# Two-layer hybrid decoder step: gate and halo tiles in a pool of their own, down pools exchanged, residual split and squares on VectorE alone, key transposes three tiles behind

## The chip, the cores and the metric

The kernel runs on one core of one Trainium2 chip. The metric is device time in microseconds (us) of one execution; lower is better. The core has a matrix engine (TensorE, PE in the profile, with weight loads PEld), VectorE (DVE), ScalarE (ACT), GpSimd (POOL) and a queue engine (SyncE, SP), which run side by side and wait for each other through semaphores. Each engine takes its own instructions strictly in order.

## The reference, cut to what matters

One inference step of a two-layer trunk, for a prompt of 1024 tokens and 64 sample tokens that share all weights. Layer 0 mixes tokens with a gated MLP and pooling, layer 1 with sliding-window attention; both then attend to 256 memory tokens and end in a convolutional feed-forward block:

```python
def rmsnorm(x, g):
    xf = x.astype(jnp.float32)
    y = xf * lax.rsqrt(jnp.mean(xf * xf, -1, keepdims=True) + EPS)
    return (y * g.astype(jnp.float32)).astype(x.dtype)

def conv_ffn(h, g_ctx, w_up, conv_w, conv_b, w_down):
    T = h.shape[1]
    up = h @ w_up
    g, u = up[..., :D_FF], up[..., D_FF:]
    g_ext = jnp.concatenate([g_ctx, g], 1)
    gc = conv_b
    for j in range(CONV_W):
        gc = gc + conv_w[j] * g_ext[:, j:j + T]
    y = (gelu(gc) * u) @ w_down
    return y, g_ext[:, -(CONV_W - 1):]

def swa_qkv(h, pos, w_qkv, q_gain, k_gain):
    N, T, _ = h.shape
    qkv = h @ w_qkv
    q = qkv[..., :N_HEADS * HEAD_DIM].reshape(N, T, N_HEADS, HEAD_DIM)
    k = qkv[..., N_HEADS * HEAD_DIM:(N_HEADS + N_KV) * HEAD_DIM].reshape(N, T, N_KV, HEAD_DIM)
    v = qkv[..., (N_HEADS + N_KV) * HEAD_DIM:].reshape(N, T, N_KV, HEAD_DIM)
    q = rope_partial(rmsnorm(q, q_gain), pos)
    k = rope_partial(rmsnorm(k, k_gain), pos)
    return q, k, v
```

D_MODEL is 1024, D_FF 2816, 16 query heads and 4 key heads of 64. The parts before and after these are not touched.

## The kernel before, in words

All 1088 tokens stay on the chip, features along partitions: 8 blocks of 128 features, by tokens in three chunks `c` of 384, 384 and 320 (`CHS`). Every fp32 operand is held as a high part (fp32r) and the remainder low part, and each product is three matmuls: high by high, high by low, low by high (L1016 to L1018 in the feed-forward block, L259 to L261 elsewhere). The residual stream lives in the tile `big`, as `xh` and `xl` for each chunk.

**Order.** TensorE's instructions stand in the order in which they are written. The other engines' instructions are put in order by the tile framework's scheduler from its own estimate, so an edit can move instructions that it does not name. A pool's tiles lie at fixed addresses in the on-chip memory (SBUF), and a new tile waits until the last users of the old tiles at its address are done.

**Feed-forward block (`ffn`).** The up projection and then the down projection run as seven-product block multiplications (`seven`, L1007): for each job seven products "1", "7", "5", "6", "4", "2", "3" in the PSUM tiles `psa` and `psb`, the products "7" and "4" of a job being run inside the next one, and at the very end alone. Between "7" and "4" the partial sum in PSUM must have been read out, since both use one tile. In the up phase the gate half goes through tiles `g` (convolution, with the two-column halo `hl`), `ge` holds the gelu, and `m` tiles hold partial results (11 buffers). Results go to DRAM tiles `hd` by SP's queue (L1250, L1255, L1256). Pools: `fg` has g, m and hl (L1135, L1193, L1219), `fge` has ge.

The down phase reads `hd` back, by POOL's queue: `load_b` (L1354 for the three parts stored split, L1357 for the four stored whole, which ScalarE and VectorE then split at L1358 and L1359). The first seven operand tiles lie in `big`, the next eight in the pool `db` (tiles `b`). The pool `de` holds `xr`, the old residual, loaded by SP at L1366. `de` is opened before `db`, so in SBUF `xr` takes the place of the first `g` tile, and the `b` tiles that of `g`, `m`, `hl` and `ge`. PSUM results are added to the new residual `x32` on VectorE at L1375 (named `x` in the profile).

**After the block of layer 0 (`after_ffn`, L1396).** For each chunk and feature block `split_x` copies the high part on ScalarE (L292), subtracts on GpSimd for even `m` and on VectorE for odd `m` (L293), squares on ScalarE (L303) and adds the square to `acc` on GpSimd for odd `m` and VectorE for even `m` (L305): 24 subtractions and 21 additions, 12 of each on GpSimd. While the down phase ends, VectorE also splits the first attention weights (L255 in `load_rows`).

**Attention of layer 1 (`swa`, L1445).** For each of nine token tiles `kv_tile` projects keys and values: 24 matmuls, then the norm's sum (`norm_tm`, L341, from `acc`), then on ScalarE the scaling (L1498) and squares (L618), on VectorE and GpSimd the head norm and rotary part (L620 to L625, L336, L1485 to L1488, tile `pT`). `trk(t - 2)` transposes the rotated keys of the tile two before on TensorE (L167), after the 18th matmul of tile t. Then come the query tiles (`q_tile`, tile `gq`): the first holds `trk(7)` in its middle, and `trk(8)` follows the second.

Of the kernel before, what the change touches and what calls it, by code (L numbers as in the profile page):

```python
# [9 lines left out]
F32 = mybir.dt.float32  # L10
F32R = mybir.dt.float32r
AF = mybir.ActivationFunctionType
ALU = mybir.AluOpType
# [10 lines left out]
HT = 544  # L24
# [47 lines left out]
def kernel(  # L72
# [10 lines left out]
    V, S, P, T = nc.vector, nc.scalar, nc.gpsimd, nc.tensor  # L83
    mm = T.matmul

    def pool(name, bufs=1, **kw):
        return tc.tile_pool(name=name, bufs=bufs, reuse_waits="tile", **kw)
# [7 lines left out]
    def f(ap):  # L95
        return ap.bitcast(F32)
# [176 lines left out]
    def proj_tm(ws, t, mid=None):  # L273
        c, o, w = tile_of(t)
        ps = psA()
        for k in range(KB):
            wt = ws[k // 2]
            mm3(ps[:w, :], xh[c][:, k, o:o + w], xl[c][:, k, o:o + w], wt[:, 0, k % 2, :], wt[:, 1, k % 2, :],
                k == 0, k == KB - 1)
            if k == 5 and mid:  # L280
                mid()
        return ps
# [4 lines left out]
    def new_acc(c, place):  # L287
        acc[c] = R["tmp"].tile([128, CHS[c][1]], F32, tag=f"acc{c}", name=f"acc{c}") if place is None else place

    def split_x(c, m, src, alt=False):  # L290
        n = CHS[c][1]
        S.activation(xh[c][:, m, :], src, AF.Copy)  # L292
        (P if alt and m % 2 == 0 else V).tensor_tensor(out=xl[c][:, m, :], in0=src, in1=f(xh[c][:, m, :]), op=ALU.subtract)  # L293
        squares(c, m, src)

    def squares(c, m, src, place=None, odd=1):
        n = CHS[c][1]
        if m == 0:
            new_acc(c, place)
            S.activation(acc[c], src, AF.Square)  # L300
        else:
            sq = tmp()
            S.activation(sq[:, :n], src, AF.Square)  # L303
            E = P if m % 2 == odd else V
            E.tensor_tensor(out=acc[c], in0=acc[c], in1=sq[:, :n], op=ALU.add)  # L305
# [815 lines left out]
    def ffn(l, xq, rvq, gtail, B0, factors, rs):  # L1121
# [10 lines left out]
        with ExitStack() as es:  # L1132
            bq = es.enter_context(tc.tile_pool(name=f"fb{l}", bufs=1, reuse_waits="tile", side="right"))
            B = [B0, {i: bq.tile([128, 2, 4, QT], F32R, name=f"b1{i}") for i in "1562374"}]
            gpp = es.enter_context(pool(f"fg{l}"))  # L1135

            def up_w(pair, up):
# [51 lines left out]
            def gate_out(pair, q):  # L1189
                hb = 2 * pair  # L1190
                g, t = [], {}
                for i in range(2):
                    gt = gpp.tile([128, 562], F32, tag="g", name="g", bufs=3)  # L1193
                    g.append(gt)

                def put(i, nh, a, b2):

                    def op(out, a_, b_):
                        if b_ is None:
                            S.activation(out, a_, AF.Copy)  # L1200
                        else:
                            V.tensor_tensor(out=out, in0=a_, in1=b_, op=ALU.add)

                    if nh == 0 or q == 0:
                        op(g[i][:, 2 + QT * nh:2 + QT * nh + QT], a, b2)
                    else:
                        op(g[i][:, 274:482], a[:, 0:208], b2[:, 0:208])
                        op(g[i][:, 482:562].rearrange("p (n r) -> p n r", r=10)[:, :, 2:10],
                           a[:, 208:272].rearrange("p (n t) -> p n t", t=8), b2[:, 208:272].rearrange("p (n t) -> p n t", t=8))

                def start(i):
                    if q == 0:
                        V.memset(g[i][:, 0:2], 0.0)
                    else:
                        V.tensor_copy(g[i][:, 0:2], halo.pop(hb + i))

                def done(i):
                    if q == 0:
                        hl = halo[hb + i] = gpp.tile([128, 2], F32, tag="hl", name="hl", bufs=4)  # L1219
                        V.tensor_copy(hl, g[i][:, 544:546])  # L1220
                    conv(hb + i, q, g[i])

                def out(what, ps):
                    if what in ("m1", "u2", "m5"):
                        t[what] = mtile()
                        S.activation(t[what], ps, AF.Copy)
                    elif what == "m2":
                        start(0)
                        put(0, 0, ps, t["m1"])
                    elif what == "m53":  # L1230
                        put(0, 1, ps, t["u2"])
                        done(0)
                    elif what == "u3":
                        start(1)
                        put(1, 1, ps, t["m5"])
                    else:
                        put(1, 0, ps, None)
                        done(1)

                return out  # L1240
# [87 lines left out]
        xpl = rs.enter_context(tc.tile_pool(name=f"x32{l}", bufs=1, reuse_waits="tile", side="right"))  # L1328
        x32 = [xpl.tile([128, KB, HT], F32, name=f"x32_{q}") for q in range(2)]
        with ExitStack() as es:  # L1330
            ep = es.enter_context(pool(f"de{l}"))
            bq = es.enter_context(pool(f"db{l}"))
            count = [0]

            def btile():
# [60 lines left out]
    def after_ffn(l, x32, conv_out):  # L1396

        conv_out(stage)
        for c, (o, n) in enumerate(CHS):
            for m in range(KB):  # L1400
                parts_ = [(q, max(o, HT * q), min(o + n, HT * q + HT)) for q in range(2)]
                parts_ = [p_ for p_ in parts_ if p_[1] < p_[2]]
                if len(parts_) == 1:
                    q, a, b = parts_[0]
                    split_x(c, m, x32[q][:, m, a - HT * q:b - HT * q], True)
                else:
                    t = tmp()[:, :n]
                    for q, a, b in parts_:
                        S.activation(t[:, a - o:b - o], x32[q][:, m, a - HT * q:b - HT * q], AF.Copy)
                    split_x(c, m, t, True)  # L1410

    def final(x32, conv_out):
        with ExitStack() as es:
# [31 lines left out]
    def swa(wkv):  # L1445
        sc = 64.0 ** -0.5
        with ExitStack() as es:
            bp = es.enter_context(pool("swa"))
            qo = bp.tile([128, 8, 1088], F32, name="qo")
            if True:  # L1450
# [41 lines left out]

                def kv_tile(t):
                    c, o, w = tile_of(t)
                    ps = proj_tm(wkv, t, (lambda: trk(t - 2)) if t > 1 else None)
                    rt[t] = norm_tm(t, f"r{t}")
                    if t < 8:
                        S.activation(vv[:, t, :], ps[:, 256:512], AF.Copy, scale=rt[t])  # L1498
# [228 lines left out]
                for i, (t, g) in enumerate(seq):  # L1727
                    if t == 0:
                        wq = [load_rows(c_w_qkv[0], r, 512 * g, g_mix[1][:, 2 * r:2 * r + 2]) for r in range(4)]
                    def mid():  # L1730
                        if i == 0:
                            trk(7)
                        else:
                            trq(*seq[i - 1])
                        if i > 2 and seq[i - 3][0] < 8:
                            pv(*seq[i - 3])

                    q_tile(wq, t, g, mid)
                    if i == 1:
                        trk(8)  # L1740
                    if i and seq[i - 1][0] < 8:
                        scores(*seq[i - 1])
                    if i > 1 and seq[i - 2][0] < 8:
                        trp(*seq[i - 2])
# [63 lines left out]
```

## Time and profile before

| | us |
|---|---|
| median of 3 runs (lowest, highest) | 2674.52 (2674.22, 2678.75) |
| the profiled execution | 2676.4 |
| its span, first to last instruction | 2674.6 |
| TensorE busy (share of the span) | 2517.4 (94%) |
| VectorE busy | 1983.9 (74%) |
| ScalarE busy | 1227.9 (46%) |
| GpSimd busy | 480.3 (18%) |

The profile is one execution. Its views: busy time in windows; groups of instructions by line, with the mean duration; the timeline of an engine, where a bracket gives the idle time ahead of an instruction and what released it; the waits. "PEclk" is the granted clock of TensorE as a share of full speed. In a view's rows `out<-in` are the program's tile names without buffer numbers. Times in rows are us from the span's start.

### The profile page before, as it was taken

How to read it: one execution, taken by the hardware profiler on the slowest of the kernel's cores; microseconds unless marked ns; L12 is line 12 of the kernel's file. 1: busy time of each engine (PE TensorE's matmuls, PEld its weight loads, DVE VectorE, ACT ScalarE, POOL GpSimd, SP SyncE). 2: the span in 40 equal slices, each digit the busy share in tenths (PEclk: the TensorE clock that was granted, in tenths of full speed). 3: DMA queues.
4: the chain of work that ended last, by engine and by line, in shares of the span. 5: the costliest groups of instructions: out<-in, count | busy, mean ns of one | idle time of the engine just before them, and what ended most of it. 6: DMA issues, size and time to landing. Idle time of an engine off the chain costs nothing. (4 is left out here: it accounts for less than half of the span.)

```text
span 2674.6 us, 46246 instructions
## 1 busy us (share of the span) xinstructions
PE 2517.4 (94%) x17136; PEld 2324.2 (87%) x17136; DVE 1983.9 (74%) x4552; ACT 1227.9 (46%) x2687; POOL 480.3 (18%) x450
## 2 busy tenths in 40 slices
PE   8999999879999998999899989999699999998998
PEld 6898987679999998999776667877599999998998
DVE  8656965788778786888667676855888778776985
ACT  5223644354554544433546554553454545544331
POOL 3506432110000001110423343421200000001100
PEclk9999999889999999999899997999799999999999
DMA  8302112523333336654111012205324333347632
GB/s 272 103 24 70 52 48 80 173 85 130 108 123 127 101 128 204 211 196 138 51 54 39 9 34 67 79 17 178 125 90 132 96 125 119 119 152 253 235 138 87
DMA packets 229345, 305.53 MB, mean 114 GB/s; under 512 B 17793, under 2 KB 189919, under 8 KB 229118
## 3 DMA queue, kind: packets, MB, share of 16 engines
q1 hardware_dynamic: 215806, 236.82, 27.7%
q0 software_dynamic: 13312, 65.74, 6.9%
q8 instruction: 135, 2.21, 0.4%
q14 instruction: 92, 0.75, 0.1%
HBM read 217.79 MB, written 84.63 MB: 113 GB/s over the span
## 5 line engine op out<-in xcount | busy, mean ns | idle before, releaser
L1064 ACT ACTIVATE w<-st 128x512 fp32r<-128x512 f32 (+2 forms) x532 | 300.0, 572 | 399.2 <-PE psb L1018 127.6
L1065 DVE TENSOR_TENSOR w<-st,w 128x512 fp32r<-128x512 f32 (+2 forms) x532 | 326.2, 618 | 179.0 <-ACT w L1064 171.8
L1016 PE MATMUL psa<-b,w 128*128 128x272 f32 x1056 | 310.0, 294 | 41.3 <-ACT b L1100 12.9
L1017 PE MATMUL psa<-b,w 128*128 128x272 f32 x1056 | 308.3, 292 | 7.4 <-DVE b L1101 7.4
L1016 PE MATMUL psa<-big,w 128*128 128x272 f32 x1056 | 310.3, 294 | 4.2 <-DVE x L1375 2.0
L1018 PE MATMUL psa<-big,w 128*128 128x272 f32 x1056 | 309.4, 293 | 0.0
L1018 PE MATMUL psa<-b,w 128*128 128x272 f32 x1056 | 308.8, 292 | 0.0
L1017 PE MATMUL psa<-big,w 128*128 128x272 f32 x1056 | 307.9, 292 | 0.0
L1016 PEld LDWEIGHTS psa<-b,w 128*128 128x128 f32 x1056 | 201.4, 191 | 44.8 <-ACT b L1100 13.4
L1016 PE MATMUL psb<-b,w 128*128 128x272 f32 x792 | 230.6, 291 | 0.0
L1018 PE MATMUL psb<-b,w 128*128 128x272 f32 x792 | 230.5, 291 | 0.0
L1018 PE MATMUL psb<-big,w 128*128 128x272 f32 x792 | 229.5, 290 | 0.3 <-DVE w L1065 0.3
L1017 PE MATMUL psb<-b,w 128*128 128x272 f32 x792 | 229.8, 290 | 0.0
L1016 PE MATMUL psb<-big,w 128*128 128x272 f32 x792 | 229.1, 289 | 0.0
L1017 PE MATMUL psb<-big,w 128*128 128x272 f32 x792 | 228.3, 288 | 0.0
L260 PE MATMUL psa<-s,w 128*128 128x384 f32 (+1 forms) x576 | 197.2, 342 | 14.2 <-DVE s L357 13.8
L1017 PEld LDWEIGHTS psa<-b,w 128*128 128x128 f32 x1056 | 202.2, 191 | 9.4 <-DVE b L1101 9.4
L1016 PEld LDWEIGHTS psa<-big,w 128*128 128x128 f32 x1056 | 203.3, 193 | 6.2 <-DVE x L1375 2.6
L1017 PEld LDWEIGHTS psa<-big,w 128*128 128x128 f32 x1056 | 203.3, 192 | 0.0
L1018 PEld LDWEIGHTS psa<-big,w 128*128 128x128 f32 x1056 | 203.0, 192 | 0.0
L1018 PEld LDWEIGHTS psa<-b,w 128*128 128x128 f32 x1056 | 201.8, 191 | 0.0
L259 PE MATMUL psa<-s,w 128*128 128x384 f32 (+1 forms) x576 | 196.8, 342 | 5.1 <-ACT s L356 5.1
(364 smaller groups left out, 6649.5 us busy)
## 6 DMA issues: line engine op xcount, KB each, us to landing
st<-in_f_w_up_dram SPq DMA_DIRECT2D x88, 512.0 KB
hd<-big SPq DMA_DIRECT2D x264, 136.0 KB
hd<-m SPq DMA_DIRECT2D x176, 136.0 KB
big<-hd POOLq DMA_DIRECT2D x48, 408.0 KB, 6.8
st<-in_f_w_down_dram SPq DMA_DIRECT2D x48, 384.0 KB
b<-hd POOLq DMA_DIRECT2D x18, 816.0 KB, 7.0
big<-hd POOLq DMA_DIRECT2D x18, 816.0 KB, 7.4
ks<-in_m_w_kv_dram SPq DMA_DIRECT2D x16, 512.0 KB
```

The source lines that it names most:

```text
L259: mm(out, lhsT=ah, rhs=bh, start=first, stop=False)
L260: mm(out, lhsT=ah, rhs=bl, start=False, stop=False)
L1016: mm(ps[:, :QT], lhsT=wt[:, 0, k, :], rhs=bt[:, 0, k, :], start=first and k == 0, stop=False, skip_group_check=True)
L1017: mm(ps[:, :QT], lhsT=wt[:, 0, k, :], rhs=bt[:, 1, k, :], start=False, stop=False, skip_group_check=True)
L1018: mm(ps[:, :QT], lhsT=wt[:, 1, k, :], rhs=bt[:, 0, k, :], start=False, stop=k == nk_of(j) - 1, skip_group_check=True)
L1064: S.activation(t[:, 0], src, AF.Copy)
L1065: V.tensor_tensor(out=t[:, 1], in0=src, in1=f(t[:, 0]), op=ALU.subtract)
```

## The change

Four edits. (1) In `ffn` the tiles `g` and `hl` move to a pool `fa` of their own, opened ahead of `fg`, which keeps the `m` tiles. (2) In the down phase the pool `db` is opened ahead of `de`. The `b` tiles now begin where `g` begins, and `xr` lies behind them, where no tile of the up phase was. The first `b` tile to be loaded covers the addresses of the three `g` tiles alone; before, it covered a part of one `g` and four `m` tiles. (3) `split_x` subtracts on VectorE for all `m`, and `after_ffn` passes `odd=None`, so that all its additions of squares are on VectorE; `x_update`, the other caller, keeps its engines. (4) In `swa` the key transposes run three tiles behind: tile t holds `trk(t - 3)`, the first query tile holds `trk(6)`, and `trk(7)` and `trk(8)` follow the first and second query tile.

```diff
-    def split_x(c, m, src, alt=False):
+    def split_x(c, m, src, odd=1):
         n = CHS[c][1]
         S.activation(xh[c][:, m, :], src, AF.Copy)
-        (P if alt and m % 2 == 0 else V).tensor_tensor(out=xl[c][:, m, :], in0=src, in1=f(xh[c][:, m, :]), op=ALU.subtract)
-        squares(c, m, src)
+        V.tensor_tensor(out=xl[c][:, m, :], in0=src, in1=f(xh[c][:, m, :]), op=ALU.subtract)
+        squares(c, m, src, None, odd)
...
+            gap = es.enter_context(pool(f"fa{l}"))
             gpp = es.enter_context(pool(f"fg{l}"))
...
-                    gt = gpp.tile([128, 562], F32, tag="g", name="g", bufs=3)
+                    gt = gap.tile([128, 562], F32, tag="g", name="g", bufs=3)
...
-                        hl = halo[hb + i] = gpp.tile([128, 2], F32, tag="hl", name="hl", bufs=4)
+                        hl = halo[hb + i] = gap.tile([128, 2], F32, tag="hl", name="hl", bufs=4)
...
+            bq = es.enter_context(pool(f"db{l}"))
             ep = es.enter_context(pool(f"de{l}"))
-            bq = es.enter_context(pool(f"db{l}"))
...
-                    split_x(c, m, x32[q][:, m, a - HT * q:b - HT * q], True)
+                    split_x(c, m, x32[q][:, m, a - HT * q:b - HT * q], None)
...
-                    split_x(c, m, t, True)
+                    split_x(c, m, t, None)
...
-                    ps = proj_tm(wkv, t, (lambda: trk(t - 2)) if t > 1 else None)
+                    ps = proj_tm(wkv, t, (lambda: trk(t - 3)) if t > 2 else None)
...
                         if i == 0:
-                            trk(7)
+                            trk(6)
...
-                    if i == 1:
-                        trk(8)
+                    if i < 2:
+                        trk(7 + i)
```

What moves on the engines, at three places. VectorE, end of the down phase of layer 0 (`x_0`, `x_1` are the two halves of the new residual, `psa` and `psb` the PSUM tiles, `w<-st,gmt,w` the low parts of the attention weights), before:

```order
L293 TENSOR_TENSOR big<-x_0_11329,big 128x384
L1375 TENSOR_TENSOR x_0_11329<-psa,x_0_11329 128x272
L293 TENSOR_TENSOR big<-x_0_11329,big 128x384
L1375 TENSOR_TENSOR x_1_11330<-psb,x_1_11330 128x272
L1375 TENSOR_TENSOR x_1_11330<-psa,x_1_11330 128x272
L255 SCALAR_TENSOR_TENSOR w<-st,gmt,w 128x512 x2
L293 TENSOR_TENSOR big<-x_0_11329,big 128x384
L1375 TENSOR_TENSOR x_0_11329<-psa,x_0_11329 128x272
L1375 TENSOR_TENSOR x_1_11330<-psb,x_1_11330 128x272 x2
L255 SCALAR_TENSOR_TENSOR w<-st,gmt,w 128x512 x2
L293 TENSOR_TENSOR big<-x_0_11329,big 128x384
L1375 TENSOR_TENSOR x_1_11330<-psa,x_1_11330 128x272 x2
```

and now, at the same place:

```order
L293 TENSOR_TENSOR big<-x_0_11333,big 128x384 x2
L1376 TENSOR_TENSOR x_0_11333<-psa,x_0_11333 128x272
L293 TENSOR_TENSOR big<-x_0_11333,big 128x384 x2
L1376 TENSOR_TENSOR x_1_11334<-psb,x_1_11334 128x272
L1376 TENSOR_TENSOR x_1_11334<-psa,x_1_11334 128x272
L255 SCALAR_TENSOR_TENSOR w<-st,gmt,w 128x512 x2
L293 TENSOR_TENSOR big<-x_0_11333,big 128x384 x2
L1376 TENSOR_TENSOR x_0_11333<-psa,x_0_11333 128x272
L293 TENSOR_TENSOR big<-x_0_11333,big 128x384
L1376 TENSOR_TENSOR x_1_11334<-psb,x_1_11334 128x272 x2
L255 SCALAR_TENSOR_TENSOR w<-st,gmt,w 128x512 x2
L1376 TENSOR_TENSOR x_1_11334<-psa,x_1_11334 128x272
```

Ahead of the read-out of `x_1` from `psa` that follows the last pair of L255 stood four subtractions (L293), and stand seven; line 1375 is 1376 in the changed file. The squares' additions (L305) behind them are then all on VectorE.

TensorE, the end of the third key and value tile (tile 2; `pT` holds the rotated keys, `psb<-ones,acc` is the norm's sum), before:

```order
L261 MATMUL psa<-w,big 128x512
L167 MATMUL psb<-idt,pT 128x128 x2
L259 MATMUL psa<-w,big 128x512
L260 MATMUL psa<-w,big 128x512
L261 MATMUL psa<-w,big 128x512
L259 MATMUL psa<-w,big 128x512
L260 MATMUL psa<-w,big 128x512
L261 MATMUL psa<-w,big 128x512
L341 MATMUL psb<-ones,acc_14189 128x2
```

and now:

```order
L261 MATMUL psa<-w,big 128x512
L259 MATMUL psa<-w,big 128x512
L260 MATMUL psa<-w,big 128x512
L261 MATMUL psa<-w,big 128x512
L259 MATMUL psa<-w,big 128x512
L260 MATMUL psa<-w,big 128x512
L261 MATMUL psa<-w,big 128x512
L341 MATMUL psb<-ones,acc_14193 128x2
```

The first transposes of keys stand one tile later, behind the 18th matmul of tile 3.

SP's queue, the turn from the up to the down phase of layer 0 (`hd` are the DRAM tiles, their last stores; layer 1 is the same), before:

```order
L1255 DMA hd_5190<-big 128x272
L1250 DMA hd_5194<-m 128x272
L1256 DMA hd_5190<-big 128x272
L1250 DMA hd_5192<-m 128x272
L1255 DMA hd_5191<-big 128x272
L1250 DMA hd_5195<-m 128x272
L1256 DMA hd_5191<-big 128x272
L1366 DMA xr<-xq_3372 128x1088
L1366 DMA big<-xq_3371 128x1088
```

and now:

```order
L1256 DMA hd_5190<-big 128x272
L1367 DMA xr<-xq_3372 128x1088
L1251 DMA hd_5194<-m 128x272
L1257 DMA hd_5190<-big 128x272
L1251 DMA hd_5192<-m 128x272
L1256 DMA hd_5191<-big 128x272
L1251 DMA hd_5195<-m 128x272
L1257 DMA hd_5191<-big 128x272
L1367 DMA big<-xq_3371 128x1088
```

The load of `xr` is issued ahead of the last six stores instead of behind them. POOL's queue keeps its order. Beside these places the scheduler swaps some VectorE rows at the end of the memory attention of layer 1: there the last addition of squares (L305, tile `rvq`) now stands ahead of two combinations (L1106) and one split (L1101) that were ahead of it.

## The prediction

> **What bounds the kernel now.** I read the busy times first, then what TensorE waited for, then the timelines around the waits that the change touches.
>
> ```profile
> span 2674.6 us, 46246 instructions
> PE 2517.4 (94%) x17136; PEld 2324.2 (87%) x17136; DVE 1983.9 (74%) x4552; ACT 1227.9 (46%) x2687; POOL 480.3 (18%) x450
> ```
>
> TensorE is the bound: what it has to do is unchanged, so time is won only from its idle 157 us and from matmuls at a low clock. From TensorE's timeline, the places the change can reach, in order of time:
>
> ```profile
> 1049.24 0.60 PE L1016 MATMUL psa<-b,w 128*128 128x272 f32 x1 [5.03 <-DMA b<-hd]
> 1286.40 0.39 PE L1016 MATMUL psa<-big,w 128*128 128x272 f32 x1 [0.90 <-DVE x L1375]
> 1295.38 0.60 PE L1016 MATMUL psa<-b,w 128*128 128x272 f32 x1 [4.21 <-DVE x L1375]
> 1305.30 0.38 PE L341 MATMUL psb<-ones,acc 128*128 128x2 f32 x2 [0.48 <-POOL acc L305]
> 1305.54 0.48 PE L259 MATMUL psa<-w,big 128*128 128x512 f32 x1
> 1311.09 0.28 PE L341 MATMUL psb<-ones,acc 128*128 128x2 f32 x2
> 1321.82 0.66 PE L167 MATMUL psb<-idt,pT 128*128 128x128 f32 x2 [6.24 <-DVE pT L1488]
> 1331.92 0.28 PE L341 MATMUL psb<-ones,acc 128*128 128x2 f32 x2
> 1917.15 0.56 PE L341 MATMUL psb<-ones,rvq 128*128 128x2 f32 x2 [5.19 <-DVE rvq L305]
> 2414.63 0.60 PE L1016 MATMUL psa<-b,w 128*128 128x272 f32 x1 [5.24 <-DMA b<-hd]
> ```
>
> The waits at 1049 and 2414 are the turn from up to down in the two layers. Those at 1286 and 1295 are the end of layer 0's down phase, where the last products wait for VectorE to read PSUM. The wait of 6.24 us is the first key transpose, too early for its keys. A wait costs more than itself: TensorE's granted clock behind it is down.
>
> ```profile
> 1295.00:1300.00 5.00, 4.62 (x17) 4.30 (x18) 1.90 (x5) 1.32 (x5) 2.21 (x5) 0.50 0.06 14
> 1320.00:1325.00 5.00, 3.18 (x10) 2.63 (x10) 2.72 (x10) 1.31 (x3) 2.15 (x3) 0.55 0.00 0
> 2400.00:2405.00 5.00, 3.23 (x18) 3.23 (x18) 2.23 (x8) 0.96 (x2) 0.54 (x1) 0.75 0.96 315
> ```
>
> In these windows (PEclk is the third number from the end) it is 0.50 to 0.75.
>
> **Part 1, the split on VectorE alone: the end of the down phase.** From 1282.5 us VectorE has no idle time until it has read out the sum that the last product waits for, while GpSimd subtracts at its side:
>
> ```profile
> 1282.50:1295.30 12.80, 12.80 (x18) 0.92 0.12 34
> L255 DVE SCALAR_TENSOR_TENSOR w<-st,gmt,w 128x512 fp32r<-128x512 f32 x6 | 7.0, 1207 | 0.0
> L293 DVE TENSOR_TENSOR big<-x,big 128x384 fp32r<-128x384 f32 x4 | 3.8, 954 | 0.0
> L255 DVE SCALAR_TENSOR_TENSOR w<-st,gmt,w 128x512 fp32r<-128x512 f32 x2 | 1.4, 744 | 0.0
> L293 DVE TENSOR_TENSOR big<-x,big 128x320 fp32r<-128x320 f32 x3 | 1.5, 490 | 0.2 <-ACT big L292 0.2
> 1298.18 0.55 DVE L305 TENSOR_TENSOR acc<-acc,t 128x384 f32<-128x384 f32 x1
> ```
>
> The first row is VectorE's windows view, the next two its groups from 1282 to 1296; then come groups from 1240 to 1282, when GpSimd was mostly still (these subtractions are of the 320-token chunk), and an addition of 384 tokens alone, which has the operands of a 384-token subtraction. Beside GpSimd's subtractions a weight split takes 1207 ns instead of 744, a subtraction of 384 tokens 954 instead of some 550. With no GpSimd work there, six splits and four subtractions give back 6 x 0.463 + 4 x 0.404 = 4.4 us. The order puts seven subtractions ahead of that read-out instead of four: 3 x 0.55 = 1.7 us more. Net **2.7 us**: the read-out comes 2.7 us earlier, and the last product with it; the wait of 0.90 lies inside that. Bounds: if the slow durations stay, 3 x 0.954 = 2.9 us lost; if VectorE is no longer late at all, 0.90 + 4.21 = 5.1 us won. I take the fast rows, since nothing of GpSimd's is left beside them but small table products.
>
> A rule speaks against this. The Trainium skill (Perfetto Trace Analysis, Optimizing Scalar/DVE Operations) says that a saturated DVE may be relieved by giving work to another engine, even GpSimd, though it warns that these two share an SBUF read port. By its first half the part would lose the 2.9 us above; the two pairs of rows bear out its warning.
>
> **Part 2, additions on VectorE and transposes a tile later: the start of the attention.** Before, additions to one accumulator alternated between GpSimd and VectorE. The price beside GpSimd and the chain behind it:
>
> ```profile
> 1302.51 1.40 DVE L305 TENSOR_TENSOR acc<-acc,t 128x384 f32<-128x384 f32 x1 [1.51 <-POOL kgr L1474]
> 1300.00:1315.00 15.00, 14.52 (x66) 11.72 (x66) 8.52 (x11) 14.01 (x38) 13.38 (x16) 1.00 0.07 18
> 1298.73 0.49 ACT L1320 ACTIVATE st<-psb 110x384 f32<-110x384 f32 x1 [3.68 <-PE psb L167]
> 1316.76 0.47 ACT L618 ACTIVATE pT<-psa,r 128x256 f32<-128x256 f32 x1
> 1341.43 0.42 DVE L620 TENSOR_REDUCE s<-pT 128x4 f32<-128x256 f32 x1 [1.53 <-ACT pT L618]
> 1344.38 0.23 DVE L1488 TENSOR_TENSOR pT<-ra,rb 128x64 f32<-128x64 f32 x1
> ```
>
> An addition is 0.55 us alone, 1.40 beside GpSimd. Between 1300 and 1315 ScalarE is busy 14.01 of 15 us: it, copying and squaring two chunks, times the first keys, from L1320 at 1298.73 to L618's end at 1317.23. VectorE's 21 additions and the subtractions left, some 30 at 0.5 us, fit in its 18.5 us. ScalarE's stretch starts 2.7 us earlier (part 1) and loses a microsecond of waits for GpSimd, so L618 ends at 1313 to 1314. The head norm and rotary chain takes 3.2 us on VectorE where nothing disturbs it (1341.43 to 1344.61) and has one addition inside: first keys at about 1317.3.
>
> When are they needed? TensorE stopped at 1321.82 - 6.24 = 1315.58, with six matmuls of tile 2 to go; the 24 matmuls of a tile take 5.55 us (tile 1: its first at 1305.54 to its norm at 1311.09). Now it runs on: 1.4 us to the end of tile 2, 0.1 for the norm, 4.2 us for 18 matmuls of tile 3. From 1315.58 that is 1321.3, less 2.7 (part 1) and 0.5 (the wait for `acc`): 1318.1. The keys are ready, barely. So from 1315.58 to the norm of tile 3, which was 16.3 us, it takes 1.4 + 0.1 + 5.55 + 0.25 for the transposes = 7.3 us: 9.0 won (6.24 of wait, 2.8 of low clock), and the 0.48 us for `acc`: **9.5 us**. Later key transposes have more slack, as TensorE needs 5.55 us a tile and VectorE's chain 3.2. Bounds: keys 3 us late and the low clock back leave 4; 9.5 is the other end.
>
> At the end of the key tiles `trk(7)` now stands behind the first query tile and its copy on ScalarE ahead of that tile's squares:
>
> ```profile
> 1371.50 0.69 ACT L618 ACTIVATE gq<-psa,r 128x512 f32<-128x512 f32 x1 [2.88 <-DMA out_dram<-gq]
> 1376.96 0.63 PE L167 MATMUL psb<-idt,gq 128*128 128x128 f32 x4 [3.36 <-DVE gq L1488]
> ```
>
> Those squares wait 2.88 us for a store of an old `gq` tile; transposes and copy hide behind that. I cost it at nothing; without that store it would be 0.7 us.
>
> **Part 3, the pools: the two turns.**
>
> ```profile
> 1043.11 2.13 POOL L1354 DMA_DIRECT2D b<-hd  x3 [0.79 <-DVE w L1065]
> 1051.88 0.57 POOL L1354 DMA_DIRECT2D b<-hd  x1 [6.64 <-DMA hd<-big]
> 1040.83 0.38 SPq L1255 DMA_DIRECT2D hd<-big  x1
> 1042.10 0.32 SPq L1250 DMA_DIRECT2D hd<-m  x1
> 1045.03 0.42 SPq L1366 DMA_DIRECT2D xr<-xq  x1
> 1045.00:1050.00 5.00, 0.76 (x3) 0.77 (x4) 2.08 (x4) 0.66 (x1) 0.24 (x1) 0.74 1.03 349
> ```
>
> TensorE waits for the first `b` tile, issued at 1043.11 after 0.79 us for `m` tiles, and landed at 1049.24. It now needs only `g` tiles, long free: 0.79 us earlier, not more, since POOL's queue ahead of it is unchanged. `xr` moves up into the gap between 1040.83 and 1042.10, out of the stretch in which the DMA engines are full (1.03). It is 0.55 MB, at 349 GB/s 1.6 us of their time, of which some speeds up the `b` tile. Against that, the six stores and ScalarE's copy that waits for one of them come behind it. I take 1.2 us a turn, **2.4** for both; bounds 2.5 won to 1.5 lost in each.
>
> The Trainium skill (DMA: Bandwidth & Descriptors, Queues, rings and completion order) has each DMA engine alternate between the queues that hold work. By that, stores and `xr` take the same share in either order, and only the 0.79 us of issue remain, 1.6 for both; no run here separates the two.
>
> **Part 4, the reordering in layer 1.** The addition that ends the wait at 1917.15 overtakes three VectorE rows such as this one:
>
> ```profile
> 1912.20 0.43 DVE L1106 TENSOR_TENSOR tc<-hx,tc 128x272 f32<-128x272 f32 x1
> ```
>
> 3 x 0.43 = 1.3 us, and the rows come back later in the same chain: I take 0.8 us, between 0.5 lost and 1.5 won.
>
> **Sum.** 2.7 + 9.5 + 2.4 + 0.8 = 15.4 us. The profiled execution took 2676.4 us (1.8 more than its span), hence 2661.0; it was 1.9 above the median of the three runs, 2674.52, so the median should be 2659.1, rounded to **2659**.
>
> **Rivals.** (a) Saturated VectorE makes the end of the down phase longer by 2.9 us, the rest holds: 2659 + 2.7 + 2.9 = 2665. For it: 12.80 of 12.80 us busy; against it the pairs of durations. (b) The early `xr` load makes both turns 1.5 us longer: 2659 + 2.4 + 3 = 2664. For it: full DMA engines at 1045; against it the gap on SP. (c) The wait for keys only moves, to tile 3 or 4, and part 1 gives nothing: 3 us remain, 2671. (d) Slower: VectorE becomes the bound. Were its 21 additions and the second chunk's eight subtractions to cost 1.40 us each, 29 x 1.4 = 40.6 us from 1295.3, the first keys would come at 1339.5 instead of the 1320.8 at which they would then be due, a wait of 18.7 in place of 6.24: 12 lost, less 3.2 from parts 3 and 4, 2683. Up to 0.75 us each nothing waits; from 1.2 us the change loses. The row of 0.55 us speaks against it. The edits can't fail to apply: the order shows them.
>
> **Chances.** Forecast 0.73, (a) 0.08, (b) 0.10, (c) 0.06, (d) 0.03. No change is a difference within 0.2%, 5.3 us, about what a measurement of this kernel can tell: (a), (b) and the forecast are faster, 0.91; (c) 0.06 the same; 0.03 slower. The range goes down to the good ends of parts 1, 3 and 4 (5.1 + 9.5 + 5 + 1.5 = 21), 2653, and up past (a) and (b) to part 2 half won and part 1 nothing (4 + 2.4 = 6.4), 2668.
>
> **What would show it.** Right: no wait at the first key transposes, or one under 1 us; L255 near 744 ns throughout; the wait near 1295 at about 2 us; first `b` tile issued with no wait; GpSimd without L293 there. Wrong: L305 over 0.75 us, a new wait of TensorE in tiles 3 to 5, or both turns still at 5 us.

## The result, and the profile after

The changed kernel takes 2657.4 us (median of 4 runs, 2656.19 to 2659.46) beside 2674.37 for the kernel before on the same chip (4 runs, 2671.03 to 2678.75): a ratio of 0.9932, 95% interval 0.9918 to 0.9945, so 17 us or 0.7% faster. Two repetitions, on two different chips, gave 0.9927 (0.9914 to 0.9939) and 0.9933 (0.9917 to 0.995).

The page of the changed kernel, its first part:

```profile
span 2657.7 us, 46231 instructions
PE 2513.4 (95%) x17136; PEld 2319.0 (87%) x17136; DVE 1987.1 (75%) x4576; ACT 1226.4 (46%) x2687; POOL 461.2 (17%) x426
```

TensorE's busy time is 4 us less and its idle time 13 us less, at the same 17136 matmuls. Its timeline, at the places that the prediction spoke of:

```profile
1047.30 0.60 PE L1016 MATMUL psa<-b,w 128*128 128x272 f32 x1 [5.24 <-DMA b<-hd]
1293.99 0.39 PE L1016 MATMUL psa<-b,w 128*128 128x272 f32 x1 [2.31 <-DVE x L1376]
1302.76 0.28 PE L341 MATMUL psb<-ones,acc 128*128 128x2 f32 x2
1318.46 0.38 PE L167 MATMUL psb<-idt,pT 128*128 128x128 f32 x2
1363.70 0.63 PE L167 MATMUL psb<-idt,gq 128*128 128x128 f32 x4 [1.75 <-DVE gq L1489]
1903.69 0.56 PE L341 MATMUL psb<-ones,rvq 128*128 128x2 f32 x2 [1.18 <-DVE rvq L305]
2401.43 0.60 PE L1016 MATMUL psa<-b,w 128*128 128x272 f32 x1 [4.84 <-DMA b<-hd]
```

The first key transposes (1318.46) have no bracket: the 6.24 us are gone, and so is the wait for `acc` at the norm. The wait at the end of the down phase is 2.31 us instead of 0.90 and 4.21. The two turns still wait 5.24 and 4.84 us. The nine matmuls behind the wait at the end of the down phase, in the kernel before and then in the changed kernel (windows view: behind the window's length stands TensorE's busy time, and the granted clock is the third number from the end):

```profile
1295.38:1297.58 2.20, 2.20 (x9) 2.20 (x10) 0.00 (x0) 0.00 (x0) 1.08 (x3) 0.50 0.03 9
1293.99:1295.25 1.26, 1.26 (x9) 1.26 (x10) 0.81 (x2) 1.26 (x5) 0.50 (x2) 0.97 0.50 157
```

At the end of the down phase VectorE's groups, and, behind the attention's start, ScalarE and VectorE:

```profile
L255 DVE SCALAR_TENSOR_TENSOR w<-st,gmt,w 128x512 fp32r<-128x512 f32 x6 | 4.2, 743 | 0.0
L293 DVE TENSOR_TENSOR big<-x,big 128x384 fp32r<-128x384 f32 x8 | 4.2, 550 | 0.0
```
```profile
1312.86 0.47 ACT L618 ACTIVATE pT<-psa,r 128x256 f32<-128x256 f32 x1
1317.04 0.23 DVE L1489 TENSOR_TENSOR pT<-ra,rb 128x64 f32<-128x64 f32 x1
```

The weight splits are back at 743 ns (1207 before), the subtractions at 550 (954). The first keys are there at 1317.27, and TensorE takes them at 1318.46.

**Where the time went, stage by stage.** A single pair of profiles mixes the change with chance, so the table uses eight profiles beside the one of the kernel before. For two matmuls that both traces hold, it gives the time between them less that of the kernel before (us; negative is faster). The stretch is named by its times in the kernel before. Old pools: `lag`, `split`, `subs`, `nopools` (below); new pools: `pools` and the three profiles of the changed kernel.

| stretch of before | lag | split | subs | nopools | pools | changed kernel, three profiles |
|---|---|---|---|---|---|---|
| 10 to 1041.5, untouched | -3.0 | -1.8 | -4.7 | -3.3 | -2.4 | -2.8, -2.7, -4.6 |
| 1041.5 to 1049.2, first turn | +0.3 | +0.4 | -0.1 | +1.1 | +0.3 | +0.4, +0.1, +0.3 |
| 1049.2 to 1075, behind it | -1.7 | -0.4 | -0.6 | -0.3 | -2.6 | -3.9, -3.7, -3.8 |
| 1098 to 1160 | -1.0 | -1.9 | -2.3 | +3.0 | 0.0 | +7.0, -1.6, -2.3 |
| 1285 to 1297.4, end of the down phase | 0.0 | -3.9 | -3.9 | -3.9 | -0.5 | -3.9, -3.9, -3.9 |
| 1297.4 to 1333, first key tiles | -8.4 | -3.4 | -0.5 | -9.7 | 0.0 | -9.6, -10.6, -10.9 |
| 1369 to 1380, first query tile | -1.2 | +0.1 | +0.6 | -0.7 | -0.9 | -1.3, -0.9, -1.3 |
| 1585 to 1680, memory attention | +1.5 | -4.6 | -3.6 | -0.3 | +2.0 | -1.0, -0.4, +1.5 |
| 1900 to 1925, `rvq` | +0.5 | +1.1 | +1.2 | 0.0 | +0.3 | -0.8, -1.0, -0.1 |
| 2404 to 2440, second turn and behind | -0.3 | -1.8 | -2.1 | +0.3 | -2.4 | -3.0, -2.1, -2.6 |

The first row says how far to trust the others: every other profile is 2 to 5 us faster there than the one profile of the kernel before, with nothing changed in the instructions. The row at 1285 repeats to a tenth among kernels with the same subtractions, but for `pools`, where the clock fell later behind a wait of the same 4.20 us; the row at 1297 repeats to about 1 us.

### The profile page after: what moved, and what is told of

Read it like the earlier page. It is cut to its first block, busy times and chain, and to the rows that moved or that the text cites. A ratio compares the mean times of both kernels' runs of the same rounds, so it can differ in the third digit from the quotient of the medians.

```text
span 2657.7 us, 46231 instructions
## 1 busy us (share of the span) xinstructions
PE 2513.4 (95%) x17136; PEld 2319.0 (87%) x17136; DVE 1987.1 (75%) x4576; ACT 1226.4 (46%) x2687; POOL 461.2 (17%) x426
## 4 chain that ended last, share of the span: by engine, by line
issue 34%; PE 28%; DVE 9%; DMA 4%; ACT 2%; POOL 1%; SPq 0%; POOLq 0%; ACTq 0%; DVEq 0%
PE psa L1016 3%; PE psa L259 3%; PE psa L1017 3%; PE psa L1018 3%; PE psa L260 3%; PE psa L261 3%; PE psb L1016 2%; PE psb L1018 2%; PE psb L1017 2%; DVE s L357 1%; DMA st<-in_f_w_down_dram 1%; DMA big<-hd 1%; PE psb L167 1%; PE psa L167 1%; PE psb L1560 1%
```

## The experiments

Theory A: the parts add up on TensorE's path as forecast (GpSimd's neighbourhood makes VectorE slow at the end of the down phase; the distance of the transposes decides the wait for keys; the pools help at the turns). Its rivals stand in each expectation as B. Ratios are to the kernel before, run beside on the same chip, with 95% intervals.

**`lag`: edit 4 alone.**

```diff
-                    ps = proj_tm(wkv, t, (lambda: trk(t - 2)) if t > 1 else None)
+                    ps = proj_tm(wkv, t, (lambda: trk(t - 3)) if t > 2 else None)
...
```

> The kernel before with edit 4 alone: key transposes three tiles behind, residual split and pools as before. Theory A (the distance of the transposes decides the wait for the keys, the split only makes them certain): TensorE needs the first keys 5.6 us later, at about 1321.3 on the clock of the kernel before, and VectorE has them at 1321.8 as before; a wait of 0.5 to 1 us is left of 6.24, the low clock behind it goes too: 8 to 9 us won, 2666. The wait of 4.21 at the end of layer 0's down phase and the turns stay. Theory B (VectorE's lateness decides, the split on VectorE is what removes the wait): the wait moves to tile 3 and is still 3 us or more; 3 us won, 2671.

Measured 0.9966 (0.9953 to 0.9979), 9 us faster. TensorE's timeline:

```profile
1292.39 0.59 PE L1016 MATMUL psa<-b,w 128*128 128x272 f32 x1 [4.20 <-DVE x L1375]
1318.85 0.41 PE L167 MATMUL psb<-idt,pT 128*128 128x128 f32 x2 [0.59 <-DVE pT L1488]
```

A holds: 0.59 us is left of 6.24, the end of the down phase is as it was, and 8.4 us are won in the stretch.

**`split`: edit 3 alone.**

```diff
-        (P if alt and m % 2 == 0 else V).tensor_tensor(out=xl[c][:, m, :], in0=src, in1=f(xh[c][:, m, :]), op=ALU.subtract)
-        squares(c, m, src)
+        V.tensor_tensor(out=xl[c][:, m, :], in0=src, in1=f(xh[c][:, m, :]), op=ALU.subtract)
+        squares(c, m, src, None, odd)
...
```

> The kernel before with edit 3 alone: subtractions and additions of squares on VectorE, transposes two tiles behind, pools as before. Theory A: weight splits (L255) at the end of the down phase at 744 ns instead of 1207, the wait of 4.21 us there at about 2.3, 2.7 us won with a little more for the clock; first keys 4.5 us earlier, but TensorE needs them 3.2 us earlier too, so a wait of about 4.9 is left of 6.24: 4 to 5 us won in all, 2670. Theory B: the keys come in time once VectorE has all additions; the wait for pT is below 1 us and 11 to 12 us are won, 2663.

Measured 0.9962 (0.9948 to 0.9977), 10 us faster:

```profile
1289.60 0.39 PE L1016 MATMUL psa<-b,w 128*128 128x272 f32 x1 [2.31 <-DVE x L1375]
1312.76 0.66 PE L167 MATMUL psb<-idt,pT 128*128 128x128 f32 x2 [5.75 <-DVE pT L1488]
```

The wait for keys is 5.75 us, so B is out: without the lag TensorE comes earlier by as much as the keys do. At these two places 7.3 us are won, more than A's 4 to 5; its profile is also 4.6 us faster in the stretch from 1585, far from the edit (last section).

**`subs`: the subtractions of edit 3 alone**, additions still alternating.

```diff
-        (P if alt and m % 2 == 0 else V).tensor_tensor(out=xl[c][:, m, :], in0=src, in1=f(xh[c][:, m, :]), op=ALU.subtract)
+        V.tensor_tensor(out=xl[c][:, m, :], in0=src, in1=f(xh[c][:, m, :]), op=ALU.subtract)
```

> The kernel before with one half of edit 3: all subtractions on VectorE, additions of squares still alternating with GpSimd. Theory A (the subtractions alone cause the contention at the end of the down phase, the alternating additions the late keys): the end of the down phase 3.9 us shorter, as with the whole of edit 3; additions that alternate do not run side by side, yet VectorE's subtractions run beside GpSimd's additions and take 0.9 us and more; the wait for the first keys 5.5 to 8 us; 2 to 4 us won in all, 2671. Theory B (additions are what makes VectorE late everywhere): the wait at the end of the down phase stays over 3.5 us, nothing won.

Measured 0.997 (0.9959 to 0.998), 8 us faster; its profile is again faster in the stretch from 1585, by 3.6 us:

```profile
1286.69 0.39 PE L1016 MATMUL psa<-b,w 128*128 128x272 f32 x1 [2.31 <-DVE x L1375]
1295.94 0.38 PE L341 MATMUL psb<-ones,acc 128*128 128x2 f32 x2 [1.95 <-POOL acc L305]
1312.03 0.66 PE L167 MATMUL psb<-idt,pT 128*128 128x128 f32 x2 [4.20 <-DVE pT L1488]
```

The subtractions alone give the whole 3.9 us at the end of the down phase. The additions belong to the key tiles: while they alternate, the norm waits 1.95 us for `acc`. My 5.5 to 8 us for the keys were too many (4.20).

**`dummy`: the changed kernel with GpSimd's twelve subtractions added again**, into a tile that nobody reads.

```diff
+        if odd is None and m % 2 == 0:
+            P.tensor_tensor(out=R["dum"][:, :n], in0=src, in1=f(xh[c][:, m, :]), op=ALU.subtract)
         squares(c, m, src, None, odd)
...
```

> The changed kernel, to which GpSimd's twelve subtractions are added again, with a result that nobody reads (VectorE does its own 24 as in the changed kernel). Theory A (GpSimd's subtraction beside VectorE is what made VectorE's rows long): L255 back from 743 to about 1200 ns, L293 from 550 to about 950; six splits and eight subtractions make 6 us, so the wait at the end of the down phase is 7 to 8 us instead of 2.31, and additions beside the last four such subtractions take over 1 us: 6 to 9 us slower than the changed kernel, 2663 to 2667. Theory B (the time before came from the order and the waits between the two engines): VectorE's rows stay at 743 and 550 ns, 2657 within 1.

Measured 0.9979 (0.9965 to 0.9994), some 13 us slower than the changed kernel, more than the 6 to 9 expected. GpSimd's timeline, then VectorE's, then TensorE's:

```profile
1275.42 1.02 POOL L295 TENSOR_TENSOR dum<-x,big 128x384 f32<-128x384 f32 x1 [56.51 <-ACT big L292]
1276.72 3.89 POOL L295 TENSOR_TENSOR dum<-x,big 128x384 f32<-128x384 f32 x3 [0.27 <-ACT big L292]
1298.47 2.71 POOL L295 TENSOR_TENSOR dum<-t,big 128x384 f32<-128x384 f32 x2
```
```profile
1276.97 2.76 DVE L255 SCALAR_TENSOR_TENSOR w<-st,gmt,w 128x512 fp32r<-128x512 f32 x2
1283.39 1.40 DVE L255 SCALAR_TENSOR_TENSOR w<-st,gmt,w 128x512 fp32r<-128x512 f32 x2
1298.46 0.54 DVE L293 TENSOR_TENSOR big<-t,big 128x384 fp32r<-128x384 f32 x1
1298.93 1.37 DVE L307 TENSOR_TENSOR acc<-acc,t 128x384 f32<-128x384 f32 x1
1300.23 1.37 DVE L293 TENSOR_TENSOR big<-t,big 128x384 fp32r<-128x384 f32 x1
1301.52 0.55 DVE L307 TENSOR_TENSOR acc<-acc,t 128x384 f32<-128x384 f32 x1
```
```profile
1288.97 0.39 PE L1018 MATMUL psa<-b,w 128*128 128x272 f32 x1 [2.31 <-DVE x L1378]
1316.96 0.66 PE L167 MATMUL psb<-idt,pT 128*128 128x128 f32 x2 [4.81 <-DVE pT L1491]
```

Read the rows against each other: two weight splits take 2.76 us while GpSimd subtracts and 1.40 when it is still; an addition or subtraction takes 1.37 us inside GpSimd's stretch from 1298.47 to 1301.18 and 0.55 on either side of it. That the slowness of these rows comes from what GpSimd does at the same time, and not from handing tiles over, is shown: no engine waits for these subtractions, and rows of the same queue are fast where GpSimd is still. The place was expected wrongly. GpSimd ran its first four at once and was done by 1280.6, so the wait at the end of the down phase stayed 2.31 us (1.94 came back ahead of it); the additions became late instead, and TensorE waits 4.81 us for the keys.

Not all of the 4.81 us is VectorE's slowness. GpSimd also makes tables that the rotary part reads, in the changed kernel early and here behind the added subtractions (changed kernel first):

```profile
1295.80 1.75 POOL L1474 TENSOR_TENSOR tabs<-tabs,kgr 128x144 f32<-128x144 f32 x3
1315.26 1.07 POOL L1476 TENSOR_TENSOR tabs<-tabs,kgr 128x144 f32<-128x144 f32 x3
```

Here they fall into the chain from the end of the first squares (L620 here, L618 in the changed kernel) to the first keys, which takes 5.94 us (1310.87 to 1316.81) instead of 3.94 (1313.33 to 1317.27). So up to 2 us of the wait may come from the order in which GpSimd now works; no run separates the two.

The Trainium skill (SBUF — State Buffer, SBUF: two separate sides) states that VectorE and GpSimd share one pair of ports as a lock that is held for a whole instruction, also by a VectorE operation with two SBUF inputs. The trace agrees as far as it goes. Side by side, two subtractions of GpSimd take 2.71 us and two rows of VectorE 2 x 1.37, where one alone takes 1.02 and 0.55; and where VectorE's row begins first (1298.46, 0.54 us), GpSimd's beside it is the long one, 1.42 us.

**`pools`: edits 1 and 2 alone; `nopools`: edits 3 and 4 alone.** The diffs are those parts of the change.

> The kernel before with edits 1 and 2 alone: tiles g and hl in a pool of their own and the two down pools exchanged. The profile of the whole change shows both turns as long as before (5.24 and about 5.2 us), but the waits of 1.87 and 0.54 us behind the turn of layer 0 gone. Theory A (the fourth b tile is loaded 5.8 us earlier because its place no longer waits for a store, so the weights behind it land earlier too): turns still 5.0 to 5.3, the waits near 1066 gone, about 2 us won in each layer, some of it lost again later in layer 0: 2 to 4 us in all, 2671. Theory B (what is won behind the turn is given back, since the down phase of layer 0 waits for its transfers anyway): within 1 us of the kernel before, 2674.

> The changed kernel with the pools of the kernel before (edits 3 and 4 alone; the last addition of squares of layer 1 stands late again here, as in the kernel before). Theory A (the pools and the reordering are worth what they won behind the turns, about 2 us a layer): the stretch from the turn to 26 us behind it as long as in the runs with the old pools, 2.5 us longer than with the new ones in layer 0, and the ratio to the kernel before 0.994 to 0.996. Theory B (all that counts is at the start of the attention; what the pools win is given back further on): 0.9925 to 0.9935, as the changed kernel.

Measured 0.9993 (0.9981 to 1.0006) and 0.9952 (0.9939 to 0.9965). In `pools` the profile is as A said (turns of 5.21 and 5.09 us, the waits near 1066 gone, though one of 1.45 us at 1054 is new), but the time, 2 us less, can't be told from nothing, so A and B stay undecided there. `nopools` is in A's range. Against the changed kernel (0.9927 to 0.9933) their absence costs 0.0019 to 0.0025, 5 to 7 us, with intervals that touch or overlap. The table says where: 3.5 us behind the first turn, 2.8 at and behind the second. Other profiles with the old pools are nearer to the new ones: `lag` behind the first turn (-1.7), `split` and `subs` at the second (-1.8, -2.1). Here is the first turn without the new pools (`nopools`), on GpSimd, ScalarE and TensorE:

```profile
1040.59 2.13 POOL L1354 DMA_DIRECT2D b<-hd  x3 [0.79 <-DVE w L1065]
1050.49 0.57 POOL L1354 DMA_DIRECT2D b<-hd  x1 [7.77 <-DMA hd<-big]
```
```profile
1062.36 0.42 ACT L1064 ACTIVATE w<-st 128x256 fp32r<-128x256 f32 x1 [3.58 <-DMA st<-in_f_w_down_dram]
```
```profile
1047.69 0.60 PE L1016 MATMUL psa<-b,w 128*128 128x272 f32 x1 [6.09 <-DMA b<-hd]
1064.48 0.39 PE L1016 MATMUL psa<-b,w 128*128 128x272 f32 x1 [1.63 <-ACT x L1373]
1066.05 0.60 PE L1016 MATMUL psa<-big,w 128*128 128x272 f32 x1 [0.54 <-DVE x L1375]
```

And with them (the second profile of the changed kernel; `issue` in a bracket means that the profile shows nothing that was waited for):

```profile
1040.37 2.13 POOL L1355 DMA_DIRECT2D b<-hd  x3
1045.93 0.57 POOL L1355 DMA_DIRECT2D b<-hd  x1 [3.44 <-issue]
```
```profile
1059.19 0.42 ACT L1064 ACTIVATE w<-st 128x256 fp32r<-128x256 f32 x1 [0.16 <-DMA st<-in_f_w_down_dram]
```

The fourth `b` load no longer stands 7.77 us behind a store of `hd`. It and the loads behind it on the queue go out some 4.3 us earlier, counted from the three loads ahead of them. The next weights are issued by SP at the same time in both (1055.41 and 1055.67 us), yet they are there when ScalarE asks for them (a wait of 0.16 us instead of 3.58), and TensorE's two waits near 1065 are gone. That the weights land earlier because GpSimd's loads are out of their way fits these rows; it was not tried by itself. The wait of the turn itself is 4.55 to 6.26 us in all ten turns with the old pools and 3.44 to 5.24 in fourteen with the new ones, `hold` and `best` left aside: in layer 0 the means differ by 0.2 us, in layer 1 by 0.7, with single turns spread by 1.5 us and more.

**`hold`: the changed kernel with the first `xr` load of each down phase held back.**

```diff
+                    if q == 1 and mp == 0:
+                        V.tensor_copy(xr[:, 0, 0:1], x32[1][:, 2, 0:1])
                     nc.sync.dma_start(out=xr, in_=xq[q][:, 2 * mp:2 * mp + 2, :])
```

> The changed kernel, with the first xr load of each layer's down phase held back until a value of the second block of weights has been added (a VectorE copy of one column into xr ahead of the load; two small instructions more): 0.56 MB less among the transfers while TensorE waits for the first b tile. Theory A (the early xr load eats what the earlier issue of the first b tile won): both turns shorter, from 5.24 and about 5.1 us to 3.6 to 4.6 us, 1 to 2 us won in each. Theory B (the b tile gets its share of the DMA engines whatever xr does): both waits stay between 5.0 and 5.5, no difference.

Measured 0.9916 (0.9901 to 0.9932), beside 0.9927 for the changed kernel on that chip: no difference that can be told. Neither theory's numbers came: the waits are 5.89 and 3.67 us. The turns, and GpSimd at the first of them:

```profile
1045.51 0.59 PE L1016 MATMUL psa<-b,w 128*128 128x272 f32 x1 [5.89 <-DMA b<-hd]
2388.65 0.60 PE L1016 MATMUL psa<-b,w 128*128 128x272 f32 x1 [3.67 <-DMA b<-hd]
```
```profile
1037.79 2.13 POOL L1355 DMA_DIRECT2D b<-hd  x3
1041.65 0.57 POOL L1355 DMA_DIRECT2D b<-hd  x1 [1.73 <-DVE b L1360]
```

Theory A falls for layer 0: with 0.56 MB less in the way the first `b` tile takes 7.72 us from issue to landing (1037.79 to 1045.51), beside 6.78 in the second profile of the changed kernel (1040.37 to 1047.15). But the removal wasn't clean: the fourth load, 816 KB where `xr` is 544, now goes out 1.7 us behind the three others instead of 3.4, and takes the place of `xr`. What sets the landing of that tile stays open. For its neighbour the traces do tell: the last load of `big` ahead of the three takes 3.3 to 3.7 us to land in the five profiles with the old pools and 3.5 in `hold` and `best`, but 5.0 to 5.4 in the seven with the early `xr`. TensorE does not wait for that one.

**`after2` and `after3`: the changed kernel repeated.**

> The changed kernel once more, on the chip that runs the next three. In its first profile two waits in the middle of layer 0's down phase (2.69 us for big from hd at 1098.74, 4.91 us for x at 1156.81, behind weights that landed late) cost about 7 us that neither the run with the pools alone nor the run with the added subtractions shows, though their instructions there are the same. Theory A (chance of one execution in the landing of transfers): both waits near 1.0 and 1.8 us here, the stretch as long as in the kernel before, and the ratio to the kernel before a little below the first one, 0.990 to 0.994. Theory B (the pools cause it): both waits again over 2.5 us.

> The changed kernel again, on the chip of the three others, to compare them with: a ratio to the kernel before of 0.991 to 0.9945; waits of 2.31 us at the end of the down phase and below 0.5 us at the first key transposes, as in its two profiles before.

Measured 0.9927 and 0.9933, both with 2.31 or 2.30 us at the end of the down phase; the first key transposes wait 0.39 us in one and not at all in the other. The two long waits in the middle of layer 0's down phase did not return as a rule (0.68 and 2.61 us in the one, 1.63 and 0.91 in the other), so theory B is out and the +7.0 in the table belongs to one execution; `hold` (+2.8) and `nopools` (+3.0) show that this stretch varies.

**`whalf`, `wlast`, `best`: weight splits moved behind the read-out.** At the end of the down phase six weight splits (4.2 us) are left in VectorE's queue beside the subtractions. `whalf` emits the last two weight blocks behind `after_ffn`, `wlast` only the last, `best` is `whalf` with `hold`.

```diff
-                wkv = [load_rows(c_w_qkv[0], r, 1024, g_mix[1][:, 2 * r:2 * r + 2]) for r in range(4)]
+                wkv = [load_rows(c_w_qkv[0], r, 1024, g_mix[1][:, 2 * r:2 * r + 2]) for r in range(2)]
                 after_ffn(0, x32, conv_out)
+                wkv += [load_rows(c_w_qkv[0], r, 1024, g_mix[1][:, 2 * r:2 * r + 2]) for r in range(2, 4)]
```

> The changed kernel, with the last two of the four blocks of key and value weights loaded and split behind the residual split in program order: of the six weight splits (L255) ahead of the read-out at the end of layer 0's down phase four stand behind it. Theory A (VectorE's queue alone makes that wait): 4 x 0.7 = 2.8 us less work ahead of the read-out, the wait of 2.31 us at 0 and the clock behind it not lowered, while the first key tile waits for the moved splits by less than 1 us: 2 to 4 us less between the end of the down phase and the second tile's norm. Theory B (the wait only moves to the first key tile, which needs the moved splits): a new wait of 2 us or more for w there, no gain.

> The changed kernel, with only the last of the four blocks of key and value weights behind the residual split in program order: two of the six weight splits (L255) go behind the read-out. Theory A: the wait of 2.31 us at the end of the down phase falls by 1.3 to 1.8 to about 0.5 to 1.0 us, and the block, needed only by the last quarter of the first key tile, makes no wait there over 0.3 us: 1 to 2 us won in that stretch. Theory B (as when two blocks were moved, the wait only moves): as much as is won comes back as a wait for w in the first key tile.

> Both edits of the two runs before, together. If theory A holds in both, 4 to 7 us below the changed kernel, about 2652 where that takes 2657; if the xr load does not matter, 2 to 4 us; if neither does, the same.

Measured 0.9918 (0.9904 to 0.9931), 0.9934 (0.992 to 0.9947) and 0.9939 (0.9926 to 0.9952), beside the changed kernel's 0.9927 for the first and the third and 0.9933 for the second. TensorE in `whalf`, then in `wlast`:

```profile
1286.03 0.39 PE L1016 MATMUL psa<-b,w 128*128 128x272 f32 x1 [0.53 <-DVE x L1376]
1293.45 0.50 PE L260 MATMUL psa<-w,big 128*128 128x512 f32 x1 [1.95 <-DVE w L255]
```
```profile
1281.51 0.39 PE L1016 MATMUL psa<-b,w 128*128 128x272 f32 x1 [0.98 <-DVE x L1376]
1289.11 0.50 PE L260 MATMUL psa<-w,big 128*128 128x512 f32 x1 [1.42 <-DVE w L255]
```

B holds in both: what is taken from the wait for the read-out comes back as a wait for the low parts of the weights in the first key tile. So these rows cost TensorE about as much at the two other places as at their own. No version beat the changed kernel by more than the measurement can tell.

## Why the prediction was right, point by point

2659 was forecast and 2657.4 measured; the mechanism of parts 1 and 2 was right. Part 3 failed: time was won around the turns, but not by the term that the sum had for it, and the prediction's own sign of being wrong, both turns still at 5 us, came true (5.24 and 4.84).

- **Part 1, end of the down phase, 2.7 us.** The durations came as taken (743 and 550 ns), and the two waits of 5.11 us became 2.31: 2.8 us. The stretch gave 3.9 us in every kernel with the subtractions on VectorE, `dummy` aside. The term left out is the clock, which the prediction names and does not price here: the nine matmuls behind the wait took 2.20 us at a granted clock of 0.50 and take 1.26 at 0.97. It now falls behind them (0.50 from 1295.25 to 1297.00). `subs` shows that the subtractions alone do this, `dummy` that GpSimd's work at the same time makes such rows long. Of the two things that the Trainium skill says there (Perfetto Trace Analysis, Optimizing Scalar/DVE Operations), the warning that moving work between these two engines might not help is the one that the runs bear out: taking the subtractions back won 3.9 us.
- **Part 2, first key tiles, 9.5 us.** Measured 9.6, 10.6 and 10.9. L618 was to end at 1313 to 1314 and ended at 1313.33, the first keys were to come at about 1317.3 and came at 1317.27. That they agree so closely is luck: the changed kernel's trace reaches the matmuls ahead of this stretch 1.65 us later (the one at 1282.33 in the kernel before comes at 1283.98), so the keys came 6.1 us earlier, not 4.5, mostly because part 1 gave more than its 2.7 us. "Ready, barely" is right: 0, 0.39 and 0 us of wait. `lag` shows that the distance takes most of it (8.4 us); the split removes the 0.59 us that `lag` leaves for the keys and the wait for `acc` (0.48 us in the kernel before, 1.25 in `lag`).
- **The first query tile, nothing.** The stretch is 0.9 to 1.3 us shorter. Of the ten profiles with edit 4 nine are 0.7 to 1.4 us shorter there than the kernel before, of the three others without it one (`pools`, 0.9). So the edit may be worth up to 1 us here; the runs do not separate it.
- **Part 3, the turns, 2.4 us.** This step failed: the 1.2 us a turn, made of 0.79 us of earlier issue and a share of `xr`'s 1.6 us, did not come off the wait for the first `b` tile. In layer 0 that tile was issued with no wait, as forecast, and landed no earlier for it: 6.97 us from issue to landing instead of 6.13, so the 0.79 us were eaten. Over all profiles the turn's wait is 0.2 us shorter in layer 0 and 0.7 in layer 1. What the pools won lies behind the turn, through a load that the prediction did not look at: the fourth `b` tile's wait of 6.64 us for a store stood in its quoted rows, and its cause was not looked for. The size of the whole is between 2 us (`pools`, alone) and 5 to 7 (`nopools`), with wide intervals. The Trainium skill's rule of alternating queues (DMA: Bandwidth & Descriptors, Queues, rings and completion order) left the 0.79 us of issue a turn; that did not show in layer 0, the 0.7 us of layer 1 would fit it but lie within the spread, and `hold` was no clean test of it.
- **Part 4, `rvq`, 0.8 us.** The wait of 5.19 us fell to 1.18 and 0.87, but new waits of 0.9 to 1.6 us for `big` stand ahead of it. The stretch gave 0.8, 1.0 and 0.1 us; other kernels vary there by as much, so this term is not shown.
- **The rivals.** (a) and (c) did not occur. (b) did not occur as a longer turn; whether the early `xr` or the loads beside it ate the earlier issue in layer 0 is open. (d) did not occur, but `dummy` shows its mechanism at work: with additions at 1.37 us a wait of 4.81 us for the keys is back, up to 2 us of it perhaps from GpSimd's order.

That 2659 and 2657.4 lie so close is partly luck. The forecast gain was 15.4 us, and the three comparisons give 17 to 21; part 1 was sized too small, and part 3's term stood for another gain of about its size or more. The parts tried alone (`lag` 9, `split` 10, `pools` 2 us) add up to 21, of which 4.6 are `split`'s stretch far from its edit.

## What to carry to other kernels

Where two engines share the work on one queue's critical stretch, compare the duration of the same row with the neighbour busy and still before counting what the sharing saves: here GpSimd's help of 0.55 us a row cost VectorE 0.8 us. A wait for a product that is made a fixed distance ahead is best removed by distance, and moving the producer forward alone does little if the consumer moves with it. When an address conflict at a turn is removed, look at every load in the queue that the conflict held, not only at the first one that the consumer waits for.

## What the runs showed of the hardware that I had not expected

- A VectorE operation on 128x384 fp32 beside a GpSimd subtraction takes 1.37 us instead of 0.55, its own time and most of the 1.02 us that GpSimd's row takes alone.
- Removing 0.79 us ahead of the first `b` load of layer 0, and 0.56 MB beside it, did not bring its landing forward: 5.5 to 7.1 us from issue to landing in the five profiles with the old pools, 6.6 to 7.0 in the seven with the new ones, 7.4 and 7.7 in `best` and `hold`.
- A wait of much the same length does not always cost the same clock: behind 4.21 us the nine matmuls took 2.20 us in the kernel before, behind 4.20 us 1.68 in `pools`.
- In the stretch from 1585 to 1680 `split`, `subs`, `hold` and `whalf` were 3.6 to 6.2 us faster than the kernel before and the nine other profiles between 1.0 faster and 2.0 slower. These four, and no other, have two loads of the value cache (`k` from `in_cache_swa_v`) earlier in SP's queue, a by-product of the scheduler. It was not tried by itself, so the cause is not shown. It also flatters `hold` and `whalf`: `best`, which has both edits and not this order, is at 0.9939.
